# Priorities, a moved softmax scaling, two reordered products and later row factors in a two-layer hybrid transformer kernel

## The chip, the cores and the metric

The kernel runs on one core of a Trainium2 chip. The metric is the device time of one execution in microseconds (us), lower is better. A measurement of this kernel can tell about 0.2% from no change.

## The reference

The program computes two transformer layers on x of 256 rows by 1024. Each layer is a SwiGLU feed-forward block (FFN, inner width 2816), a mixer, and another FFN, each between two RMS norms and added to x. Layer 0 has the even mixer: latent attention (four heads, keys and queries of 128 + 64 rotated columns) beside a gated linear recurrence. Layer 1 has the odd mixer: differential attention, eight heads with two score maps each.

```python
for l in range(DEPTH):                                   # DEPTH = 2
    h = swiglu(rms_norm(x, g[0, 0]), w_gate, w_up, w_down); x = x + 0.5 * rms_norm(h, g[0, 1])
    h = rms_norm(x, g[1, 0])
    m = even_mixer(h, ...) if l % 2 == 0 else odd_mixer(h, ...)
    x = x + rms_norm(m, g[1, 1])
    h = swiglu(rms_norm(x, g[2, 0]), w_gate, w_up, w_down); x = x + 0.5 * rms_norm(h, g[2, 1])
# even attention: o = softmax(mask((q_nope @ k_nope.T + q_rope @ k_rope.T) * scale)) @ v
# odd attention:  p = softmax(s_0) - lam * softmax(s_1);  o = rms_norm(p @ v, g_head) * (1 - lambda_init)
```

(The listing is shortened; weights of the layers have their own names.)

## The kernel before

The 256 rows are two tiles of 128, t=0 and t=1. Every weight comes from HBM in pieces of 128 by 1024 floats (512 KB), issued by SyncE. ScalarE rounds a piece into `whi` (L269), VectorE subtracts to get the rest `wlo` (L274), and each product is three matmuls (`mm3`, L294 to L296: hi by hi, hi by lo, lo by hi). Activations are turned by TensorE (`to_T`, transposes at L403), copied as hi by ScalarE (`split`, L410) and as rest by VectorE (L411). The first product after a norm is `group_first` (matmuls at L342); it takes the second tile's turned halves as `turn1`.

Mixers are built from `group` calls, and between the pieces of weights of one group a function `pump` calls one step of the list `side`: a rope, a turn, a block of scores, a softmax. TensorE thus always has weight products around the small steps, and the order of work on each engine is the program's order, except that the scheduler places what stands in `tc.high_priority()` earlier on its engine. Before the change that holds for `split` and `post_norm` alone.

What the change touches:

- `finish` (L453) ends a block: `post_norm` of tile 0, the pieces left, `rms_x(0)`, `post_norm` of tile 1, `rms_x(1)`. `rms_x` squares a whole tile on ScalarE (L421), rounds off on VectorE (L391) and raises to the power -1/2 on GpSimd (L393). Its result r[t] is the factor with which the next block scales its first products (for instance L809 and L816 in the even mixer).
- Even mixer: `after_cq(t)` squares `cq` (L809), makes `kp` (L816) out of the same PSUM bank, `turn_cq` turns it. The table E of the recurrence comes by a DMA that ScalarE issues (L782), and ScalarE rounds it into `W` (L783). `scores(t)` makes four heads with two matmuls each, L931 (128 rows of contraction) and L932 (64 rows), then VectorE's maximum, ScalarE's exponentials and, on GpSimd, the scaling by the row sums (L940).
- Odd mixer: `after_z` scales and ropes a group's output (L1117 to L1120, rope at L717 to L720), `turn_z` turns it (L1127), `scores` makes the maps (L1144), the maxima (L1148), exponentials (L1152), the scaling of the second map on GpSimd (L1156) and the difference of the maps on VectorE (L1158), `turn_p` turns the result (L1169), `attend` multiplies by v (L1179) and applies the head norm (squares L1182, product L1188), `turn_o` turns that into the last product's operand (`to_T`).

Of the kernel before, what the change touches and what calls it, by code (L numbers as in the profile page):

```python
# [20 lines left out]
P = 128  # L21
# [162 lines left out]
def forward(ctx, tc, a):  # L184
# [268 lines left out]
    def finish(ys, gpost, half, gnext, pieces, at):  # L453


        xg = post_norm(0, ys[0], gpost, half, gnext)
        turns = turn_x(0, xg)
        for i, p in enumerate(pieces):
            if gnext is not None and i in at:
                turns[at.index(i)]()  # L460
            p()
        r0 = rms_x(0) if gnext is not None else None
        xg = post_norm(1, ys[1], gpost, half, gnext)
        if gnext is None:
            return None, None
        return [r0, rms_x(1)], turn_x(1, xg)


    def ffn_scope(block):
# [299 lines left out]
    def even(r, turn1, tab, lb, lbm):  # L769
        with ExitStack() as ex:  # L770
# [149 lines left out]
            def scores(t):  # L920
                nk = (t + 1) * P
                per = 512 // nk
                pm = one.tile([P, 4, nk], F32, name=f"pm{t}", tag=f"pm{t}")
                pms[t] = pm
                mx, nb, ssum, rs = small(4), small(4), small(4), small(4)
                for h0 in range(0, 4, per):
                    sc = ybank()
                    v = sc.rearrange("p (h k) -> p h k", h=per)
                    for i in range(per):
                        h = h0 + i  # L930
                        mm(v[:, i, :], qT[t][:, h, :], knT[:, h, :nk], start=True, stop=False)  # L931
                        mm(v[:, i, :], qrT[t][:, h, :], kpeT[:, :nk], start=False, stop=True)  # L932
                    nc.vector.memset(v[0:64, :, nk - 64:nk], -1e31)
                    nc.vector.tensor_reduce(mx[:, h0:h0 + per], v, axis=AX.X, op=ALU.max)
                    nc.vector.tensor_scalar(nb[:, h0:h0 + per], mx[:, h0:h0 + per], -scale, None, op0=ALU.mult)
                    for i in range(per):
                        h = h0 + i
                        nc.scalar.activation(pm[:, h, :], v[:, i, :], AF.Exp, scale=scale, bias=nb[:, h:h + 1], accum_out=ssum[:, h:h + 1])
                nc.vector.reciprocal(rs, ssum)
                nc.gpsimd.tensor_tensor(pm, pm, rs.unsqueeze(2).broadcast_to([P, 4, nk]), op=ALU.mult)  # L940

            def turn_p(t):
                for kt in range(t + 1):
                    pt = bank()
                    for h in range(4):
                        nc.tensor.transpose(pt[:, hsl[h]], pms[t][:, h, kt * P:(kt + 1) * P], ident)
                    p_ = m.tile([P, 512], F32, name="m", tag="m")
                    nc.scalar.copy(p_, pt)
                    pTs[t].append(p_)

            def attend(t):
# [139 lines left out]
    def odd(r, turn1, tab):  # L1091
        with ExitStack() as ex:
# [24 lines left out]
            def after_z(t, key, ps):  # L1117
                z = m.tile([P, 512], F32, name="m", tag="m")
                nc.scalar.activation(z, ps, AF.Copy, scale=r[t])
                rope(z.rearrange("p (n d) -> p n d", d=64)[:, :, 0:16], tab[:, t], 8, m)  # L1120
                zs[t, key] = z

            def turn_z(t, key):
                which, part = key
                pt = bank()
                for h in range(4):
                    nc.tensor.transpose(pt[:, hsl[h]], zs[t, key][:, hsl[h]], ident)  # L1127
                hs = slice(part * 4, part * 4 + 4)
                dst = qT[t][:, hs, :] if which == 0 else kT[:, hs, t * P:(t + 1) * P]
                nc.scalar.copy(dst, pt.rearrange("p (h n) -> p h n", h=4))  # L1130

            pms = {}

            def scores(t, part, hl):

                nk = (t + 1) * P
                n = 512 // nk
                pm = m2.tile([P, 2, n, nk], F32, name="pm", tag="pm", bufs=3)
                mx, nb, ssum, rs = small(2 * n), small(2 * n), small(2 * n), small(2 * n)
                sc = [ybank().rearrange("p (h k) -> p h k", h=n) for _ in range(2)]  # L1140
# [4 lines left out]
                for c in range(2):
                    nc.vector.memset(sc[c][0:64, :, nk - 64:nk], -1e31)
                    ms = slice(c * n, (c + 1) * n)
                    nc.vector.tensor_reduce(mx[:, ms], sc[c], axis=AX.X, op=ALU.max)  # L1148
                    nc.vector.tensor_scalar(nb[:, ms], mx[:, ms], -scale, None, op0=ALU.mult)
                    for i in range(n):  # L1150
                        q = c * n + i
                        nc.scalar.activation(pm[:, c, i, :], sc[c][:, i, :], AF.Exp, scale=scale, bias=nb[:, q:q + 1], accum_out=ssum[:, q:q + 1])  # L1152
                nc.vector.reciprocal(rs, ssum)
                rl = small(n)
                nc.vector.tensor_scalar(rl, rs[:, n:2 * n], nlam, None, op0=ALU.mult)
# [7 lines left out]
            def turn_p(t, part, hl):  # L1163
# [6 lines left out]
                nc.vector.tensor_copy(pTs[t, part][:, 0:t + 1, hl:hl + n, :], pt.rearrange("p (k h n) -> p k h n", h=n, n=P))  # L1170

            obs = {}

            def attend(t, part):
                po = (ybank, bank)[part]()
                for hl in range(4):
                    h = part * 4 + hl
                    for kt in range(t + 1):
                        mm(po[:, hsl[hl]], pTs[t, part][:, kt, hl, :], v[kt][:, h * P:(h + 1) * P], start=kt == 0, stop=kt == t)  # L1179
                ss = small(4)  # L1180
                for h in range(4):
                    nc.scalar.activation(junk[:, hsl[h]], po[:, hsl[h]], AF.Square, accum_out=ss[:, h:h + 1])  # L1182
                k2 = 1.0 / (1.0 - LI) ** 2
                ro = rpow(ss, 4, k2 / P, EPS * k2)
                o_ = m.tile([P, 512], F32, name="m", tag="m")
                for hl in range(4):
                    gs = slice((part * 4 + hl) * P, (part * 4 + hl + 1) * P)
                    nc.vector.scalar_tensor_tensor(o_[:, hsl[hl]], po[:, hsl[hl]], ro[:, hl:hl + 1], gh[:, gs], op0=ALU.mult, op1=ALU.mult)  # L1188
# [31 lines left out]
            for part in range(2):  # L1220
# [97 lines left out]
```

## Time and profile before

| | |
|---|---|
| time, median of 3 runs | 1015.85 us (1015.84 to 1016.21) |
| profiled execution, its own time | 1009.94 us |
| its span, first to last instruction | 1008.2 us |
| TensorE (PE) busy | 990.5 us, 98% |
| VectorE (DVE) busy | 788.4 us, 78% |
| ScalarE (ACT) busy | 583.4 us, 58% |
| GpSimd (POOL) busy | 52.2 us, 61 instructions |
| granted TensorE clock | 1.00 in the whole span but the last stretch (0.98) |

PE is the matmul part of TensorE and PEld its weight loads. A busy share is the mean over the span; what an engine waits for is read stretch by stretch. Tiles have the program's names, and a wait is put down to the instruction that ended it.

### The profile page before, as it was taken

What the parts mean: (1) busy time and instruction counts of PE and PEld (TensorE: products, weight loads), DVE (VectorE), ACT (ScalarE), POOL (GpSimd) and SP (SyncE); (2) the same over time, 40 slices, a digit from 0 to 9 for tenths busy, and PEclk for the clock granted to TensorE, in tenths of its full rate; (3) what the DMA queues carried; (4) which work ended last, traced back from release to release, by engine and by line L of the source; (5) the groups of instructions that cost most, each with busy time, mean ns of one, the idle gap of its engine ahead of it and who ended that gap; (6) DMA issues with size and microseconds to landing.
All of it is one profiled execution on the core that took longest, in us unless ns stands there. A gap on an engine that the chain in (4) does not pass through costs nothing.

```text
span 1008.2 us, 13275 instructions
## 1 busy us (share of the span) xinstructions
PE 990.5 (98%) x4883; PEld 825.0 (82%) x4883; DVE 788.4 (78%) x1068; ACT 583.4 (58%) x846; POOL 52.2 (5%) x61
## 2 busy tenths in 40 slices
PE   8999999999999999999999999999999999999997
PEld 6888988888788888888888889888877788889886
DVE  5998996578567899888479988865776779988852
ACT  5746584377644755657447474744665657474731
POOL 1000000021202000000010000000010210000000
PEclk9999999999999999999999999999999999999999
DMA  8938273375223883827456392737634357292701
GB/s 349 374 113 295 70 255 116 105 260 184 99 69 119 312 288 104 305 68 266 175 200 233 113 306 80 271 117 259 230 125 137 119 171 244 95 304 85 252 1 42
DMA packets 51905, 184.26 MB, mean 183 GB/s; under 512 B 6136, under 2 KB 6528, under 8 KB 51840
## 3 DMA queue, kind: packets, MB, share of 16 engines
q1 hardware_dynamic: 48960, 176.05, 50.7%
q10 hardware_dynamic: 2880, 7.37, 2.2%
q8 instruction: 38, 0.62, 0.3%
q14 instruction: 27, 0.22, 0.1%
HBM read 182.35 MB, written 1.05 MB: 182 GB/s over the span
## 4 chain that ended last, share of the span: by engine, by line
PE 89%; DVE 5%; ACT 2%; issue 1%; POOL 1%; DMA 1%; SPq 0%; POOLq 0%; DVEq 0%; ACTq 0%
PE w L294 16%; PE w L296 16%; PE w L295 16%; PE y L294 9%; PE y L296 9%; PE y L295 9%; PE w L342 7%; DVE wlo L274 2%; PE w L403 2%; PE w L1023 1%; ACT whi L269 1%; PE y L403 1%; DMA raw<-in_w_dram 1%; POOL pm L1156 1%; DVE pm L1158 0%
## 5 line engine op out<-in xcount | busy, mean ns | idle before, releaser
L269 ACT CAST whi<-raw 128x1024 fp32r<-128x1024 f32 (+2 forms) x379 | 391.4, 1049 | 268.7 <-PE y L296 90.3
L274 DVE TENSOR_TENSOR wlo<-raw,whi 128x1024 fp32r<-128x1024 f32 (+2 forms) x379 | 456.7, 1228 | 96.1 <-ACT whi L269 92.4
L294 PE MATMUL w<-whi,xThi 128*128 128x512 f32 (+1 forms) x676 | 252.7, 374 | 0.0
L296 PE MATMUL w<-whi,xTlo 128*128 128x512 f32 (+1 forms) x676 | 249.7, 369 | 0.0
L295 PE MATMUL w<-wlo,xThi 128*128 128x512 f32 (+1 forms) x676 | 249.3, 369 | 0.0
L296 PEld LDWEIGHTS w<-whi,xTlo 128*128 128x128 f32 x676 | 127.4, 188 | 21.9 <-issue 0.3
L294 PEld LDWEIGHTS w<-whi,xThi 128*128 128x128 f32 x676 | 127.5, 189 | 21.5 <-issue 1.0
L295 PEld LDWEIGHTS w<-wlo,xThi 128*128 128x128 f32 x676 | 127.5, 189 | 20.4
L294 PE MATMUL y<-whi,hThi 128*128 128x512 f32 x352 | 138.7, 394 | 0.0
L296 PE MATMUL y<-whi,hTlo 128*128 128x512 f32 x352 | 137.5, 391 | 0.0
L295 PE MATMUL y<-wlo,hThi 128*128 128x512 f32 x352 | 137.4, 390 | 0.0
L214 DVE TENSOR_TENSOR raw<-raw 128x1024 f32<-128x1024 f32 x64 | 77.4, 1220 | 1.0
L296 PEld LDWEIGHTS y<-whi,hTlo 128*128 128x128 f32 x352 | 66.1, 188 | 14.3
L295 PEld LDWEIGHTS y<-wlo,hThi 128*128 128x128 f32 x352 | 66.1, 188 | 13.5
L294 PEld LDWEIGHTS y<-whi,hThi 128*128 128x128 f32 x352 | 66.1, 188 | 13.5
L411 DVE TENSOR_TENSOR hTlo<-w,hThi 128x512 fp32r<-128x512 f32 (+1 forms) x48 | 29.8, 641 | 28.4 <-ACT hThi L410 28.0
L438 POOL TENSOR_TENSOR sm<-sm,mhalf 128x1 f32<-128x1 f32 x12 | 6.6, 550 | 701.7 <-DVE sm L436 701.7
L342 PE MATMUL w<-whi,xThi 128*128 128x512 f32 (+2 forms) x124 | 39.0, 393 | 3.9 <-ACT xThi L410 3.9
L410 ACT CAST hThi<-w 128x512 fp32r<-128x512 f32 (+1 forms) x48 | 25.1, 552 | 24.5 <-PE w L403 24.5
L342 PE MATMUL w<-wlo,xThi 128*128 128x512 f32 (+2 forms) x124 | 37.4, 387 | 0.4 <-DVE wlo L274 0.4
L342 PE MATMUL w<-whi,xTlo 128*128 128x512 f32 (+2 forms) x124 | 37.7, 385 | 0.0
L492 ACT ACTIVATE s<-w,sm 128x512 f32<-128x512 f32 (+1 forms) x40 | 25.9, 647 | 15.8 <-PE w L296 15.6
(276 smaller groups left out, 1158.1 us busy)
## 6 DMA issues: line engine op xcount, KB each, us to landing
raw<-in_w_dram SPq DMA_DIRECT2D x325, 512.0 KB, 5.6
g<-in_norm_g_dram ACTq DMA_DIRECT2D x9, 512.0 KB, 5.8
raw<-in_w_dram SPq DMA_DIRECT2D x4, 448.0 KB, 4.1
g<-in_norm_g_dram SPq DMA_DIRECT2D x2, 512.0 KB, 8.5
out_dram<-x SPq DMA_DIRECT2D x4, 256.0 KB, 2.0
E<-in_hw_dram ACTq DMA_DIRECT2D x1, 576.0 KB, 6.8
x<-in_x_dram SPq DMA_DIRECT2D x2, 256.0 KB, 3.1
x<-in_x_dram SPq DMA_DIRECT2D x1, 512.0 KB
```

Of the source, the lines that this page charges most:

```text
L214: nc.vector.tensor_tensor(to, to, what, op=ALU.add)
L269: c = nc.scalar.copy(hi[:, :w], raw[:, :w])
L274: state["lo"] = nc.vector.tensor_tensor(lo[:, :w], raw[:, :w], hi[:, :w].bitcast(F32), op=ALU.subtract)
L294: mm(ps, hi[:, j, :], rhi, start=start, stop=False, skip_group_check=again)
L295: mm(ps, hi[:, j, :], rlo, start=False, stop=False, skip_group_check=again)
L296: state["mm"] = mm(ps, lo[:, j, :], rhi, start=False, stop=stop, skip_group_check=again)
L342: state["mm"] = mm(o, lhs[:, k, :], rhs[:, i, :], start=j == 0 and k == 0, stop=j == 2 and k == KD - 1)
L403: nc.tensor.transpose(ps[:, i * P:(i + 1) * P], src[:, (b + i) * P:(b + i + 1) * P], ident)
L410: c = nc.scalar.copy(h2, ps)
L411: return c, nc.vector.tensor_tensor(lo.rearrange("p a b -> p (a b)"), ps, h2.bitcast(F32), op=ALU.subtract)
L492: nc.scalar.activation(s[:, :w], ps[:, :w], AF.Silu, scale=r[t])
L1023: mm(o, e, e, start=True, stop=True)
```

## The change

Six edits. The row factors: `finish` runs `rms_x(t)` after each half of the next block's second-tile turn, and `ffn` makes the negated factors after its first group. High priority stands on the even mixer's turn copies, query rope and softmax, and on the odd mixer's rope, turn copies, softmax and head norm. The scaling of exponentials leaves GpSimd: in the even mixer 8 ScalarE copies with a scale take the place of 2 GpSimd products, in the odd one 16 VectorE products the place of 6. The two matmuls of an even head come in alternating order from head to head. Odd attention of (t=0, part 1) comes before that of (1, 1), and so do their turns.

```diff
@@ finish
-        r0 = rms_x(0) if gnext is not None else None
         xg = post_norm(1, ys[1], gpost, half, gnext)
...
-        return [r0, rms_x(1)], turn_x(1, xg)
+        r = [None] * NT
+        def then(t, f):
+            def go():
+                f()
+                r[t] = rms_x(t)
+            return go
+        return r, [then(t, f) for t, f in enumerate(turn_x(1, xg))]
@@ ffn
-            nr = [small() for _ in range(NT)]
-            for t in range(NT):
-                nc.vector.tensor_scalar(nr[t], r[t], -1.0, None, op0=ALU.mult)
+            nr = []
...
             h = [gated(t, pu[t], s[t], w) for t in range(NT)]
+            for t in range(NT):
+                nr.append(small())
+                nc.vector.tensor_scalar(nr[t], r[t], -1.0, None, op0=ALU.mult)
@@ even, turn4 (turn_p and the query rope likewise)
-                (copy or nc.scalar.copy)(dst, pt[0:rows, :].rearrange("p (h n) -> p h n", h=4))
+                with tc.high_priority():
+                    (copy or nc.scalar.copy)(dst, pt[0:rows, :].rearrange("p (h n) -> p h n", h=4))
@@ even, scores
-                        mm(v[:, i, :], qT[t][:, h, :], knT[:, h, :nk], start=True, stop=False)
-                        mm(v[:, i, :], qrT[t][:, h, :], kpeT[:, :nk], start=False, stop=True)
+                        pair = [(qT[t][:, h, :], knT[:, h, :nk]), (qrT[t][:, h, :], kpeT[:, :nk])][::1 - 2 * (h % 2)]
+                        for j, (lhs, rhs) in enumerate(pair):
+                            mm(v[:, i, :], lhs, rhs, start=j == 0, stop=j == 1)
...
-                nc.gpsimd.tensor_tensor(pm, pm, rs.unsqueeze(2).broadcast_to([P, 4, nk]), op=ALU.mult)
+                for h in range(4):
+                    nc.scalar.activation(pm[:, h, :], pm[:, h, :], AF.Copy, scale=rs[:, h:h + 1])
@@ odd, after_z (turn_z, the whole softmax, turn_p's copy and attend's head norm likewise)
-                rope(z.rearrange("p (n d) -> p n d", d=64)[:, :, 0:16], tab[:, t], 8, m)
+                with tc.high_priority():
+                    rope(z.rearrange("p (n d) -> p n d", d=64)[:, :, 0:16], tab[:, t], 8, m)
@@ odd, scores (all of it now in the high priority block)
-                nc.gpsimd.tensor_tensor(pm[:, 1, :, :], pm[:, 1, :, :], rl.unsqueeze(2).broadcast_to([P, n, nk]), op=ALU.mult)
-                for i in range(n):
-                    nc.vector.scalar_tensor_tensor(pm[:, 0, i, :], pm[:, 0, i, :], rs[:, i:i + 1], pm[:, 1, i, :], op0=ALU.mult, op1=ALU.add)
+                    for i in range(n):
+                        nc.vector.tensor_scalar(pm[:, 1, i, :], pm[:, 1, i, :], rl[:, i:i + 1], None, op0=ALU.mult)
+                        nc.vector.scalar_tensor_tensor(pm[:, 0, i, :], pm[:, 0, i, :], rs[:, i:i + 1], pm[:, 1, i, :], op0=ALU.mult, op1=ALU.add)
@@ odd, the last steps
-            side.extend([seq((attend, 1, 1), (attend, 0, 1)), None, seq((turn_o, 1, 1)), seq((turn_o, 0, 1))])
+            side.extend([seq((attend, 0, 1), (attend, 1, 1)), None, seq((turn_o, 0, 1)), seq((turn_o, 1, 1))])
```

The order of SyncE's queue does not change. Three places of the order follow, before and then now; lines of the changed kernel have moved down by 8 to 20.

First ScalarE at the front of the even mixer, where `junk,sm<-x` is the square of `rms_x`, `junk,sm<-w,sm` that of `cq` (128x384, one for each tile), `cqThi` the turned `cq`, and E and W the recurrence's table and its rounded copy.

```order
L809 ACTIVATE junk,sm<-w,sm 128x384
L269 CAST whi<-raw 128x1024 x2
L816 ACTIVATE kp<-w,sm 128x64
L410 CAST cqThi<-y 128x384
L809 ACTIVATE junk,sm<-w,sm 128x384
L782 DMA E<-in_hw_dram 128x1152
L816 ACTIVATE kp<-w,sm 128x64
L410 CAST cqThi<-y 128x384
L809 ACTIVATE junk,sm<-w,sm 128x256
L269 CAST whi<-raw 128x1024
L783 CAST W<-E 128x1152
```

```order
L421 ACTIVATE junk,sm<-x_89 128x1024
L269 CAST whi<-raw 128x1024
L818 ACTIVATE junk,sm<-w,sm 128x384
L269 CAST whi<-raw 128x1024
L790 DMA E<-in_hw_dram 128x1152
L410 CAST cqThi<-y 128x384
L825 ACTIVATE kp<-w,sm 128x64
L421 ACTIVATE junk,sm<-x_90 128x1024
L269 CAST whi<-raw 128x1024
L818 ACTIVATE junk,sm<-w,sm 128x384
L791 CAST W<-E 128x1152
L825 ACTIVATE kp<-w,sm 128x64
```

Both squares of `rms_x` moved in here from further up, the issue of E's DMA now stands ahead of the first `kp`, and the second `kp` moved behind the cast of W.

Then TensorE in the odd mixer, at the scores of (t=1, part 1, heads 2 and 3), between `attend` of (0, 0) and the products of the last group.

```order
L1179 MATMUL y<-v_6446,pT_6448 128x128 x4
L1144 MATMUL y<-kT,qT_6444 128x256 x2
L294 MATMUL w<-whi,xThi_91 128x512
L295 MATMUL w<-wlo,xThi_91 128x512
L1144 MATMUL y<-kT,qT_6444 128x256 x2
L296 MATMUL w<-whi,xTlo_92 128x512
```

```order
L1197 MATMUL y<-v_6440,pT_6442 128x128 x4
L1160 MATMUL y<-kT,qT_6438 128x256 x4
L294 MATMUL w<-whi,xThi_91 128x512
L295 MATMUL w<-wlo,xThi_91 128x512
L296 MATMUL w<-whi,xTlo_92 128x512
```

The four score products were split by two weight matmuls and now stand together.

Last TensorE at the end of the odd mixer: `y<-whi,oThi` and `y<-whi,xThi` are the last product's matmuls by the first and the second part of the attention's output (95 and 91 belong to t=0, 97 and 93 to t=1), and L403 from `m` is `turn_o`.

```order
L403 MATMUL w<-ident,m 128x128 x4
L294 MATMUL y<-whi,oThi_97 128x512
L295 MATMUL y<-wlo,oThi_97 128x512
L296 MATMUL y<-whi,oTlo_98 128x512
L294 MATMUL y<-whi,oThi_97 128x512
L295 MATMUL y<-wlo,oThi_97 128x512
L296 MATMUL y<-whi,oTlo_98 128x512
L294 MATMUL y<-whi,xThi_91 128x512
```

```order
L403 MATMUL w<-ident,m 128x128 x4
L294 MATMUL y<-whi,oThi_95 128x512
L295 MATMUL y<-wlo,oThi_95 128x512
L296 MATMUL y<-whi,oTlo_96 128x512
L294 MATMUL y<-whi,oThi_95 128x512
L295 MATMUL y<-wlo,oThi_95 128x512
L296 MATMUL y<-whi,oTlo_96 128x512
L403 MATMUL w<-ident,m 128x128 x4
L294 MATMUL y<-whi,xThi_91 128x512
```

Before, the turn of (0, 1) was the second one (the first row above) and stood six matmuls ahead of its first use; now it is the first, with six matmuls and the other turn between it and that use.

## Rows read from the trace of the kernel before

**Rows 1.** Page, part 1: busy time of each engine.
```profile
PE 990.5 (98%) x4883; PEld 825.0 (82%) x4883; DVE 788.4 (78%) x1068; ACT 583.4 (58%) x846; POOL 52.2 (5%) x61
```

**Rows 2.** Windows: busy us (instructions) of PE, PEld, DVE, ACT, POOL; clock; DMA share; GB/s.
```profile
200.00:230.00 30.00, 30.00 (x171) 26.25 (x170) 21.51 (x39) 21.44 (x36) 9.73 (x8) 1.00 0.74 241
250.00:290.00 40.00, 40.00 (x213) 32.11 (x213) 22.20 (x54) 21.68 (x44) 5.62 (x6) 1.00 0.31 103
740.00:760.00 20.00, 17.68 (x88) 13.52 (x89) 18.42 (x48) 12.59 (x28) 4.23 (x3) 1.00 0.39 132
```

**Rows 3.** Waits of PE: total us, times, longest us.
```profile
PE w L342 <- ACT xThi L410: 3.9, 2, 2.9
PE w L1127 <- DVE sm L1149: 1.4, 1, 1.4
...
PE y L294 <- ACT xThi L410: 1.4, 1, 1.4
PE w L1169 <- DVE pm L1158: 0.9, 1, 0.9
...
PE y L931 <- DVE knT L799: 0.6, 1, 0.6
PE w L403 <- DVE m L1188: 0.6, 1, 0.6
```

**Rows 4.** Timeline of PE, even scores and attend: start, us, what [idle before].
```profile
248.56 0.46 PE L931 MATMUL y<-knT,qT 128*128 128x128 f32 x2 [0.60 <-DVE knT L799]
...
251.86 0.66 PE L798 MATMUL w<-ident,kk 128*128 128x128 f32 x4
...
255.10 0.59 PE L931 MATMUL y<-knT,qT 128*128 128x256 f32 x2
...
260.01 0.44 PE L798 MATMUL w<-ident,kk 128*128 128x128 f32 x2
...
277.85 1.95 PE L955 MATMUL w<-m,va 128*128 128x128 f32 x16
279.63 0.60 PE L798 MATMUL w<-ident,m 128*128 128x128 f32 x4
```

**Rows 5.** Timeline of ACT, front of the even mixer; last row, third FFN's start.
```profile
211.91 0.34 ACTq L782 DMA_DIRECT2D E<-in_hw_dram  x1
...
213.77 0.31 ACT L816 ACTIVATE kp<-w,sm 128x64 f32<-128x64 f32 x1 [0.92 <-DVE m L810]
...
218.74 1.16 ACT L783 CAST W<-E 128x1152 fp32r<-128x1152 f32 x1 [2.24 <-DMA E<-in_hw_dram]
...
830.75 1.06 ACT L421 ACTIVATE junk<-x 128x1024 bf16<-128x1024 f32 x1 [3.18 <-DVE x L444]
```

**Rows 6.** Timeline of PE, first matmuls of the hf group.
```profile
213.16 0.40 PE L294 MATMUL w<-whi,xThi 128*128 128x512 f32 x1
213.39 0.40 PE L295 MATMUL w<-wlo,xThi 128*128 128x512 f32 x1
```

**Rows 7.** Page, part 5, VectorE: busy us, mean ns of one, idle before.
```profile
L274 DVE TENSOR_TENSOR wlo<-raw,whi 128x1024 fp32r<-128x1024 f32 (+2 forms) x379 | 456.7, 1228 | 96.1 <-ACT whi L269 92.4
```

**Rows 8.** Timeline of POOL, odd softmax.
```profile
740.01 1.04 POOL L1156 TENSOR_TENSOR pm<-pm,sm 128x512 f32<-128x512 f32 x1 [29.11 <-PE y L1144]
```

**Rows 9.** Timeline of DVE, odd softmax, and the last head norm.
```profile
740.24 1.89 DVE L274 TENSOR_TENSOR wlo<-raw,whi 128x1024 fp32r<-128x1024 f32 x1 [0.46 <-ACT whi L269]
742.05 1.13 DVE L1158 SCALAR_TENSOR_TENSOR pm<-pm,sm 128x128 f32<-128x128 f32 x4
...
756.25 0.88 DVE L1158 SCALAR_TENSOR_TENSOR pm<-pm,sm 128x256 f32<-128x256 f32 x2 [0.93 <-POOL pm L1156]
...
801.43 1.13 DVE L1188 SCALAR_TENSOR_TENSOR m<-w,sm,gh 128x128 f32<-128x128 f32 x4 [1.12 <-POOL sm L393]
```

**Rows 10.** Timeline of PE, two odd score blocks.
```profile
770.59 1.13 PE L1144 MATMUL y<-kT,qT 64*128 64x256 f32 x8
...
777.69 1.13 PE L1144 MATMUL y<-kT,qT 64*128 64x256 f32 x4 [0.40 <-ACT pm L1152]
```

More of the change, by code (lines that the diff above doesn't have):

```diff
@@ L888, in even @@
                 nc.scalar.activation(qr[t], psr[t][:, :256], AF.Copy, scale=rq[t])
-                rope(qr[t].rearrange("p (h d) -> p h d", h=4), tab[:, t], 32, m)
+                with tc.high_priority():
+                    rope(qr[t].rearrange("p (h d) -> p h d", h=4), tab[:, t], 32, m)
             def turn_q(t):
@@ L930, in scores @@
                         h = h0 + i
-                        mm(v[:, i, :], qT[t][:, h, :], knT[:, h, :nk], start=True, stop=False)
-                        mm(v[:, i, :], qrT[t][:, h, :], kpeT[:, :nk], start=False, stop=True)
[L933 to L938, printed above, removed]
+                        pair = [(qT[t][:, h, :], knT[:, h, :nk]), (qrT[t][:, h, :], kpeT[:, :nk])][::1 - 2 * (h % 2)]
+                        for j, (lhs, rhs) in enumerate(pair):
+                            mm(v[:, i, :], lhs, rhs, start=j == 0, stop=j == 1)
+                    with tc.high_priority():
+                        nc.vector.memset(v[0:64, :, nk - 64:nk], -1e31)
+                        nc.vector.tensor_reduce(mx[:, h0:h0 + per], v, axis=AX.X, op=ALU.max)
+                        nc.vector.tensor_scalar(nb[:, h0:h0 + per], mx[:, h0:h0 + per], -scale, None, op0=ALU.mult)
+                        for i in range(per):
+                            h = h0 + i
+                            nc.scalar.activation(pm[:, h, :], v[:, i, :], AF.Exp, scale=scale, bias=nb[:, h:h + 1], accum_out=ssum[:, h:h + 1])
                 nc.vector.reciprocal(rs, ssum)
-                nc.gpsimd.tensor_tensor(pm, pm, rs.unsqueeze(2).broadcast_to([P, 4, nk]), op=ALU.mult)
+                for h in range(4):
+                    nc.scalar.activation(pm[:, h, :], pm[:, h, :], AF.Copy, scale=rs[:, h:h + 1])
             def turn_p(t):
@@ L947, in turn_p @@
                     p_ = m.tile([P, 512], F32, name="m", tag="m")
-                    nc.scalar.copy(p_, pt)
+                    with tc.high_priority():
+                        nc.scalar.copy(p_, pt)
                     pTs[t].append(p_)
@@ L1119, in after_z @@
                 nc.scalar.activation(z, ps, AF.Copy, scale=r[t])
-                rope(z.rearrange("p (n d) -> p n d", d=64)[:, :, 0:16], tab[:, t], 8, m)
+                with tc.high_priority():
+                    rope(z.rearrange("p (n d) -> p n d", d=64)[:, :, 0:16], tab[:, t], 8, m)
                 zs[t, key] = z
@@ L1129, in turn_z @@
                 dst = qT[t][:, hs, :] if which == 0 else kT[:, hs, t * P:(t + 1) * P]
-                nc.scalar.copy(dst, pt.rearrange("p (h n) -> p h n", h=4))
+                with tc.high_priority():
+                    nc.scalar.copy(dst, pt.rearrange("p (h n) -> p h n", h=4))
             pms = {}
@@ L1144, in scores @@
                         mm(sc[c][:, i, :], qT[t][cs, part * 4 + hl + i, :], kT[cs, part * 4 + hl + i, :nk], start=True, stop=True)
[L1145 to L1149, printed above, removed]
-                    for i in range(n):
[L1151 to L1155, printed above, removed]
-                nc.gpsimd.tensor_tensor(pm[:, 1, :, :], pm[:, 1, :, :], rl.unsqueeze(2).broadcast_to([P, n, nk]), op=ALU.mult)
-                for i in range(n):
-                    nc.vector.scalar_tensor_tensor(pm[:, 0, i, :], pm[:, 0, i, :], rs[:, i:i + 1], pm[:, 1, i, :], op0=ALU.mult, op1=ALU.add)
+                with tc.high_priority():
+                    for c in range(2):
+                        nc.vector.memset(sc[c][0:64, :, nk - 64:nk], -1e31)
+                        ms = slice(c * n, (c + 1) * n)
+                        nc.vector.tensor_reduce(mx[:, ms], sc[c], axis=AX.X, op=ALU.max)
+                        nc.vector.tensor_scalar(nb[:, ms], mx[:, ms], -scale, None, op0=ALU.mult)
+                        for i in range(n):
+                            q = c * n + i
+                            nc.scalar.activation(pm[:, c, i, :], sc[c][:, i, :], AF.Exp, scale=scale, bias=nb[:, q:q + 1], accum_out=ssum[:, q:q + 1])
+                    nc.vector.reciprocal(rs, ssum)
+                    rl = small(n)
+                    nc.vector.tensor_scalar(rl, rs[:, n:2 * n], nlam, None, op0=ALU.mult)
+                    for i in range(n):
+                        nc.vector.tensor_scalar(pm[:, 1, i, :], pm[:, 1, i, :], rl[:, i:i + 1], None, op0=ALU.mult)
+                        nc.vector.scalar_tensor_tensor(pm[:, 0, i, :], pm[:, 0, i, :], rs[:, i:i + 1], pm[:, 1, i, :], op0=ALU.mult, op1=ALU.add)
                 pms[t, part, hl] = pm
@@ L1169, in turn_p @@
                         nc.tensor.transpose(pt[:, (kt * n + i) * P:(kt * n + i + 1) * P], pm[:, 0, i, kt * P:(kt + 1) * P], ident)
-                nc.vector.tensor_copy(pTs[t, part][:, 0:t + 1, hl:hl + n, :], pt.rearrange("p (k h n) -> p k h n", h=n, n=P))
+                with tc.high_priority():
+                    nc.vector.tensor_copy(pTs[t, part][:, 0:t + 1, hl:hl + n, :], pt.rearrange("p (k h n) -> p k h n", h=n, n=P))
             obs = {}
@@ L1179, in attend @@
                         mm(po[:, hsl[hl]], pTs[t, part][:, kt, hl, :], v[kt][:, h * P:(h + 1) * P], start=kt == 0, stop=kt == t)
[L1180 to L1188, printed above, removed]
+                with tc.high_priority():
+                    ss = small(4)
+                    for h in range(4):
+                        nc.scalar.activation(junk[:, hsl[h]], po[:, hsl[h]], AF.Square, accum_out=ss[:, h:h + 1])
+                    k2 = 1.0 / (1.0 - LI) ** 2
+                    ro = rpow(ss, 4, k2 / P, EPS * k2)
+                    o_ = m.tile([P, 512], F32, name="m", tag="m")
+                    for hl in range(4):
+                        gs = slice((part * 4 + hl) * P, (part * 4 + hl + 1) * P)
+                        nc.vector.scalar_tensor_tensor(o_[:, hsl[hl]], po[:, hsl[hl]], ro[:, hl:hl + 1], gh[:, gs], op0=ALU.mult, op1=ALU.mult)
                 obs[t, part] = o_
```

## Prediction

> **What bounds the kernel now.** First the busy times: TensorE is busy 990.5 of 1008.2 us, VectorE 788, ScalarE 583, GpSimd 52 [rows 1]. So TensorE bounds the kernel nearly everywhere, and a change that leaves the number of matmuls alone can at most take away the 17.7 us in which TensorE stands still, plus what its own instructions lose between one another. Then the windows: where a group of weights runs smoothly the idle time is nil, 30.00 of 30 us at the front of the even mixer, with the clock at 1.00; in the odd mixer's softmax stretch TensorE is busy 17.68 of 20 us while VectorE is at 18.42 [rows 2]. Then TensorE's waits by releaser: 3.9 us for `xThi` in two pieces (2.9 of it at the program's start, which the change does not touch, so 1.0 at the start of the third FFN), 1.4 for a roped tile behind the softmax, 1.4 for the last turn, 0.9 for the probabilities, 0.6 for `knT`, 0.6 for the head norm [rows 3]. Most of the rest of the 17.7 us is the program's start and end. What the change can reach is thus about 6 us of waits, and some matmul overhead.
>
> **The sum, part by part.** All terms are against the profiled execution, 1009.94 us with 1.7 us around its span; the median of the runs, 1015.85, is 5.9 higher, and I carry that difference over unchanged.
>
> *Alternating score matmuls, even mixer.* The t=0 block of 16 records takes 251.86 − 248.56 = 3.30 us, 0.206 each; 16 records of one shape, all 128 rows of contraction, take 279.63 − 277.85 = 1.78 us, 0.111 each [rows 4]. The block changes between 128 and 64 rows with every pair of records, 8 times with the change at its end, so (3.30 − 1.78) / 8 = 0.19 us for one change of shape. The t=1 block takes 260.01 − 255.10 = 4.91 us [rows 4]; with twice the columns 16 × 0.22 + 8 × 0.19 = 5.0 would be expected, which agrees. With the order alternating by head (128, 64, 64, 128, 128 and so on) 4 changes are left in each block: 8 × 0.19 = 1.5 us less, all on TensorE's path. Nought, if the loss belongs to something else than the shape.
>
> *Row factors later, even mixer's front: a new wait.* Both squares of `rms_x`, 1.06 us each [rows 5], come after the turn on ScalarE. r[0] is ready only after its square, VectorE's round-off and GpSimd's power; `cq`'s square waits for r[0], and behind that on ScalarE's queue stands the DMA of E. By the new order this DMA is ahead of both `kp`, one `cqThi` and the second `cq` square, but behind one `rms_x` square and the wait for r[0]: I put its issue at 211.0, against 211.91 before. The cast of W started 218.74 − 211.91 = 6.8 us after the issue, and its row says that it waited 2.24 us for that DMA [rows 5]. That hid, because the second `kp` had run at 213.77, 5 us ahead of it. Now the second `kp` is queued behind the cast, and its bank is what TensorE needs for the t=1 half of the hf group. Issue 211.0 + 6.8 = 217.8, cast 1.16, `kp` 0.31 [rows 5]: 219.3. TensorE starts the hf group at 213.16 with 0.23 a matmul [rows 6]; 17 t=0 matmuls now stand ahead of the first t=1 matmul, with two turns of three transposes at 0.11 [rows 4], so it wants the bank at 213.16 + 3.9 + 0.7 = 217.7. That is a stall of 1.6 us, and I add 0.2 for banks that wait for the late square: loss 1.8. The bounds: 0.3, if the DMA lands 1.5 us sooner, and 3, if r[0] holds the issue until 212.2. The DMA engines are busy 0.74 of this stretch [rows 2], so a later landing is a rival below. SyncE's queue keeps its order; on GpSimd's only the two powers move, and nothing else waits in it there.
>
> *Scaling in the even mixer to ScalarE.* Two GpSimd products go, eight scaled copies of 128 or 256 columns come on ScalarE. The nearest rows are `kp`, 64 columns in 0.31 us, and W, 1152 columns in 1.16 [rows 5], so up to 0.5 each, 4 us in all. ScalarE is busy 21.68 of 40 us from 250 to 290 [rows 2], while TensorE does weight products; I take nothing. If that cover went, the two blocks' turns would be late by up to 4 × 0.5 = 2 us each.
>
> *FFN starts.* At the FFN behind the even mixer the turns come about one cast nearer to `post_norm`: −0.4 (0 to −1). At the third FFN `rms_x` (1.06 us [rows 5]) leaves ScalarE's way to `xThi`, whose wait was 1.0 us [rows 3]; but the turns of the second tile also come earlier in TensorE's order than `post_norm` may feed them: +0.3 (−0.3 to +1.0). The other block ends show no wait and get none.
>
> *Odd softmax, 740 to 757.* GpSimd's product is a link between the exponentials and VectorE's difference: VectorE idles 0.93 us for it [rows 9], TensorE 0.9 in its wake, and 1.4 for a rope that stood behind the softmax [rows 3]. The products go to VectorE, eight of 128x128 and eight of 128x256. By the nearest rows, the differences, 1.13 / 4 = 0.28 and 0.88 / 2 = 0.44 us [rows 9], the three blocks (of six) in this stretch add 4 × 0.28 + 4 × 0.44 = 2.9 us to an engine that had 1.6 us idle in 20 [rows 2]. What it gets back: a `wlo` took 1.89 us [rows 9] while GpSimd's product of 1.04 us ran [rows 8], against a mean of 1.23 [rows 7], so 0.7 each time. Priority puts the ropes first, which removes the 1.4, and lets the probabilities come later. So VectorE is the limit with or without GpSimd, and I take 0 for the two waits (−1.0 to +1.5).
>
> The Trainium skill (Perfetto Trace Analysis, Optimizing Scalar/DVE Operations) says that where VectorE is saturated, offloading work to ScalarE or even GpSimd may make sense, which speaks against this part, and adds that between GpSimd and VectorE it might not help since they share a port. The first half is rival 2, 0.4 us in place of the sum's 2.9; the second half is what the 1.89 us row shows.
>
> *Odd scores at 777.* Four records of a block run at 777.69 after a wait of 0.40, split off from their other four; these four take 1.13 us, as long as a whole block of eight at 770.59, 1.13 [rows 10]. Together they pay it once: 0.4 + 1.1 = 1.5 us. It needs the exponentials that free their bank to come earlier, which priority gives. 0 to 1.6.
>
> *Head norm at 790.* The wait of 0.6 [rows 3] goes, since squares and products now come ahead of the weights' casts: 0.6 (0 to 1.0).
>
> *Last turns.* The turn that is used first was the second. Now six matmuls and a turn, 6 × 0.23 + 0.4 = 1.8 us, lie between it and its use, against a wait of 1.4 [rows 3]. Its cast, and `xTlo` behind two `wlo`, still follow the head norms, the second of which starts at 801.43 [rows 9]; that may leave 0.2. So 1.2 (0.3 to 1.5).
>
> The wait for `knT` stays: VectorE's order ahead of it is the old one.
>
> Sum: 1.5 − 1.8 − 0.4 + 0.3 + 1.5 + 0.6 + 1.2 = **2.9 us faster**: 1007.0 for a profiled execution, 1012.95 for the median, as a forecast 1013.0.
>
> **Rivals.**
> 1. *Slower: E's DMA.* One mechanism, W's cast ahead of the second `kp` on ScalarE. For: the order has it so, and the DMA had no slack before. If E takes twice as long (13.6 us) behind pieces of weights, the stall is 1.6 + 6.8 = 8.4 and the sum 4.7 − 8.4 − 0.2 = −3.9: 1019.7. It decides from a landing 2.9 us later than assumed, and shows as slower from 4.9. Against: the 6.8 us came in the same traffic. Chance 0.07.
> 2. *VectorE becomes the bound in the odd mixer.* Products and priority delay `wlo` and the turned probabilities; the gains at 777 and 790 (2.1) and 0.4 of the last turns do not come: 2.9 − 2.5 = 0.4, 1015.4. For: it is 92% busy from 740 to 760. Against: 0.7 back per product, and no rise of its share elsewhere. Chance 0.22.
> 3. *More: no stall at the front*, because E lands early, and 1.2 of the waits from 740 to 757 gone: 2.9 + 1.6 + 1.2 = 5.7, 1010.1. Chance 0.18.
> 4. *The shape order does nothing*, since each new pair costs by itself: 2.9 − 1.5 = 1.4, 1014.4. Chance 0.08.
>
> **How the numbers follow.** The forecast has 0.45, and the time is its own, 1013.0. The range runs from rival 3 to no gain, 1009.5 to 1016.0; outside lie rival 1 and the edges. A measurement can tell 0.2%, 2.0 us. Faster than that: most of the forecast (0.40), rival 3 (0.18), some of 4 and 2: 0.62. Within: 0.29. Slower: rival 1 and a bad end of rival 2, 0.09.
>
> **What would show it.** Right: the t=0 score block at about 2.5 us and t=1 at about 4.1; a wait of TensorE of 1 to 2 us near 217 for the second `kp`; eight odd score records in one row near 775; no wait for the head norm near 790, and under 0.5 us at the last turns; VectorE at 19 of 20 us from 740 to 760. Wrong: no wait near 217, or one of over 4 us; waits for `wlo` in the odd mixer; score blocks as long as before; a granted clock under 1.00 where it was 1.00.

## The result and the profile after

| | before | changed |
|---|---|---|
| median, first comparison (6 runs each) | 1015.45 us (1012.8 to 1016.21) | 1006.77 us (1006.18 to 1009.64) |
| ratio, 95% interval | | 0.9925 (0.9908 to 0.9943) |
| median, measured again later (e5; 19 and 5 runs) | 1012.14 us | 1007.62 us |
| ratio, 95% interval | | 0.9953 (0.9937 to 0.997) |
| profiled execution, span | 1009.94, 1008.2 us | 1009.64, 1007.8 us |

The change made the kernel faster, by 8.7 us in the first comparison and by 4.5 in the second. The forecast was 2.9 faster, a time of 1013.0, and 1006.77 lies below its range. The two profiled executions differ by only 0.3 us, so neither of the two gains is seen in them as it stands.

Busy times of the changed kernel (page, part 1, as [rows 1]) have hardly moved; only GpSimd has less to do.

```profile
PE 991.2 (98%) x4883; PEld 826.5 (82%) x4883; DVE 789.4 (78%) x1084; ACT 585.0 (58%) x854; POOL 47.8 (5%) x53
```

TensorE's waits of the changed kernel (total, times, longest us), as [rows 3]:

```profile
PE w L342 <- ACT xThi L410: 3.4, 2, 2.8
PE w L1186 <- DVE pm L1175: 2.4, 2, 2.2
...
PE y L296 <- DVE oTlo L411: 1.0, 1, 1.0
PE w L1037 <- DVE A L1039: 0.7, 1, 0.7
PE y L943 <- DVE knT L808: 0.6, 1, 0.6
...
PE w L403 <- DVE pT L1188: 0.2, 1, 0.2
PE y L296 <- DVE xTlo L411: 0.2, 1, 0.2
```

The waits for the roped tile and for the last turn's `xThi` are gone, as is the one at 832, the start of the FFN behind the odd mixer. (That is the fourth of the program's four FFNs; the prediction calls it the third.) The 3.4 us for `xThi` are 2.8 at the program's start and 0.6 at the start of the real third FFN, at 533. New are 2.2 us for probabilities (L1186) and 1.0 for `oTlo`. On TensorE's timeline, the hf group's second-tile start, the two score blocks, and the odd mixer, as [rows 4, 10]:

```profile
218.79 0.49 PE L403 MATMUL y<-ident,m 128*128 128x128 f32 x3
219.03 0.48 PE L294 MATMUL w<-whi,xThi 128*128 128x512 f32 x1
...
250.30 0.46 PE L943 MATMUL y<-knT,qT 128*128 128x128 f32 x2 [0.64 <-DVE knT L808]
...
257.74 0.60 PE L943 MATMUL y<-knT,qT 128*128 128x256 f32 x2
...
261.98 0.60 PE L806 MATMUL w<-ident,kk 128*128 128x128 f32 x4
...
759.79 0.30 PE L1186 MATMUL w<-ident,pm 128*128 128x128 f32 x1 [2.17 <-DVE pm L1175]
...
778.44 1.14 PE L1160 MATMUL y<-kT,qT 64*128 64x256 f32 x8
...
791.41 0.66 PE L403 MATMUL w<-ident,m 128*128 128x128 f32 x4 [0.24 <-DVE pT L1188]
...
795.48 0.50 PE L296 MATMUL y<-whi,oTlo 128*128 128x512 f32 x1 [0.97 <-DVE oTlo L411]
...
806.68 0.50 PE L296 MATMUL y<-whi,xTlo 128*128 128x512 f32 x1 [0.22 <-DVE xTlo L411]
```

The eight odd score records at 778.44 now run in one piece, the last turn waits 0.22. ScalarE's front of the even mixer, as [rows 5]:

```profile
211.65 0.34 ACTq L790 DMA_DIRECT2D E<-in_hw_dram  x1
...
217.25 1.16 ACT L791 CAST W<-E 128x1152 fp32r<-128x1152 f32 x1
218.50 0.31 ACT L825 ACTIVATE kp<-w,sm 128x64 f32<-128x64 f32 x1
```

E landed by 217.25 at the latest, 5.6 us after its issue, and the second `kp` ended at 218.81, just ahead of the 219.03 at which TensorE came to its bank. And VectorE ahead of the 2.2 us wait:

```profile
757.62 0.22 DVE L725 TENSOR_TENSOR rp<-m,roped 128x64 f32<-128x64 f32 x1
...
758.43 0.35 DVE L1174 TENSOR_SCALAR pm<-pm,sm 128x256 f32<-128x256 f32 x1
758.69 0.22 DVE L725 TENSOR_TENSOR rp<-m,roped 128x64 f32<-128x64 f32 x1
...
759.16 0.48 DVE L1175 SCALAR_TENSOR_TENSOR pm<-pm,sm 128x256 f32<-128x256 f32 x1
```

Ropes stand ahead of the maps' scaling (L1174) and again between it and the difference (L1175) that TensorE waits for; L725 is one of a rope's products.

That the two traces differ by 0.3 and not by 4.5 us is in part the clock (1.00 is 2.4 GHz, 0.50 is 1.2). In the changed kernel's trace the granted clock fell inside the even scores, here in windows as [rows 2]; in before's it did not.

```profile
250.00:255.00 5.00, 4.70 (x23) 4.06 (x24) 3.11 (x6) 1.68 (x3) 0.00 (x0) 0.79 0.77 265
255.00:260.00 5.00, 5.00 (x19) 3.64 (x19) 0.18 (x1) 4.99 (x16) 0.00 (x0) 0.87 0.10 38
```

At the program's start the clock column misleads. Before's windows show 1.00 there, but its first products behind the start's wait run slowly; the changed kernel (windows 10 to 20: 0.55 and 0.77) only stays slow for longer. TensorE in before, then the second of these pairs in the changed kernel:

```profile
9.76 1.22 PE L342 MATMUL w<-whi,xThi 128*128 128x512 f32 x2 [2.94 <-ACT xThi L410]
...
13.95 0.74 PE L342 MATMUL w<-whi,xThi 128*128 128x512 f32 x2
```

```profile
13.84 1.20 PE L342 MATMUL w<-whi,xThi 128*128 128x512 f32 x2
```

From the first product to the hundredth matmul record behind it before takes 24.45 us and the changed kernel 26.01.

### The profile page after: what moved, and what is told of

It is laid out like the page before. It is cut to its first block, busy times and chain, and to the rows that moved or that the text cites. A ratio compares the mean times of both kernels' runs of the same rounds, so it can differ in the third digit from the quotient of the medians.

```text
span 1007.8 us, 13278 instructions
## 1 busy us (share of the span) xinstructions
PE 991.2 (98%) x4883; PEld 826.5 (82%) x4883; DVE 789.4 (78%) x1084; ACT 585.0 (58%) x854; POOL 47.8 (5%) x53
## 4 chain that ended last, share of the span: by engine, by line
PE 89%; DVE 6%; DMA 1%; ACT 1%; issue 1%; POOL 0%; SPq 0%; DVEq 0%; POOLq 0%; ACTq 0%
PE w L294 16%; PE w L296 16%; PE w L295 16%; PE y L296 9%; PE y L295 9%; PE y L294 9%; PE w L342 7%; DVE wlo L274 2%; PE w L403 2%; DMA raw<-in_w_dram 1%; PE w L1037 1%; PE y L403 1%; PE y L943 1%; DVE sm L1165 1%; ACT whi L269 1%
## 5 line engine op out<-in xcount | busy, mean ns | idle before, releaser
L269 ACT CAST whi<-raw 128x1024 fp32r<-128x1024 f32 (+2 forms) x379 | 391.5, 1049 | 257.9 <-PE w L296 79.9
```

Of the source, the lines that this page charges most:

```text
L269: c = nc.scalar.copy(hi[:, :w], raw[:, :w])
```

## The experiments

The gains below are against runs of the kernel before that were taken beside each experiment, on the same chip. The table under the experiments tells where in the program they arise.

**e1, the kernel before again.**

> The kernel before, unchanged, to see the granted clock of its timed runs. Known: its one profiled execution took 1009.94 us with the clock at 1.000, its timed runs 1012.8 to 1016.2; the changed kernel's runs took 1006.2 to 1009.6 with mean clocks of 0.993 to 0.998. Theory C (clock): of the 8.7 us, some 3.4 are waits and shape changes and the rest is the clock, which falls to half for some us after waits that the change removes; then most runs here show mean clocks of 0.985 to 0.993 with spans of 1011 to 1014, and a run at 1.000 has a span near 1008. Theory W (waits): the clock is as in the changed kernel, 0.993 to 0.998, and the spans are above 1010 all the same, because waits differ from run to run.

1012.01 against 1011.73 us: the same; here the kernel before is 3.7 us faster than it was first. Mean clocks 0.992 to 1.000, most of them 0.995 or 0.996. Neither theory holds as put: the clock is as in the changed kernel, but it does sort the runs. In all the experiments together the kernel before was run 99 times: the 22 runs with a mean clock up to 0.994 have a median of 1013.9 us, the 62 at 0.995 to 0.997 of 1011.7, the 15 above of 1011.0.

**e2, e3, e4: one part each.** e2 has only the edits in `finish` and `ffn`, e3 only those of the even mixer, e4 only those of the odd mixer, each as the diff above has them.

> Only the later row factors. In the trace of the changed kernel the second kp came in time (no wait near 217) and the FFN starts changed by -1 to +1 us. Theory C: within 1 us of before, mean clocks as before. Theory W: 0.3 to 1 us faster from the third FFN's start, less the 0.6 us wait that the changed kernel has at 533.

> Only the even mixer's edits (priority, alternating score matmuls, scaling on ScalarE). Both theories: 1.3 us faster, all from the score blocks (3.30 to 2.6 and 4.91 to 4.2 us). Theory C adds that the mean clock stays as in the kernel before, since the wait for knT stays.

> Only the odd mixer's edits (priority, scaling on VectorE, last turns). The traces give 3.2 us less waiting from 740 to 815. Theory C: 5 to 7 us faster in the timed runs, with a mean clock some 0.003 to 0.006 higher than the kernel before shows in e1. Theory W: 3.2 us faster at the same clock.

e2: 0.7 us faster (ratio 0.9992, 0.9983 to 1.0), which both theories allow. e3: 1.2 (0.9987, 0.9978 to 0.9995), as both said. e4: 1.5 (0.9981, 0.997 to 0.9993), with a mean clock up to 0.994 in 7 of 12 runs: behind its 2.2 us wait near 760 the clock fell in the profile to 0.88 and 0.78 of full in two 5 us stretches. Theory C said 5 to 7 us for e4, and lost; theory W's 3.2 missed too, in the trace by 1.6 us that the fall cost.

**e5, the changed kernel again; e8, without the row factors** (`finish` and `ffn` as before).

> The changed kernel, unchanged, beside the kernel before. The three parts alone gave 0.7, 1.2 and 1.5 us, 3.4 in sum, and the mean clock was 0.992 to 1.000 with the edits and without, so theory C of the first runs has lost. Theory A (the parts add up; what was seen first, 8.7 us, holds a difference of the kernel before between chips or hours, 1015.4 there against 1011.7 here): 3 to 4.5 us faster, ratio 0.9955 to 0.997. Theory I (the parts work together, each alone leaves a wait that the next one takes over): 7 to 9 us faster, ratio near 0.992.

> The changed kernel without the later row factors. Theory A: 0 to 1 us slower than the changed kernel (0.7 alone), the score of the even front 0.3 us better, the third FFN's wait of 1 us back, and the 0.6 us wait near 533 gone. Theory I: 2 us slower or more.

e5: 4.5 us faster, theory A. e8: 1007.45, the same as e5: inside the changed kernel the later row factors are worth nothing that can be told. Against what was expected of e8, the wait of 1 us at the fourth FFN did not come back.

**e6, no priority on the odd rope.**

```diff
-                with tc.high_priority():
-                    rope(z.rearrange("p (n d) -> p n d", d=64)[:, :, 0:16], tab[:, t], 8, m)
+                rope(z.rearrange("p (n d) -> p n d", d=64)[:, :, 0:16], tab[:, t], 8, m)
```

> The changed kernel without the priority on the odd mixer's rope alone. The changed kernel's largest new wait is 2.17 us near 760 for the probabilities of (1, 0, heads 2 and 3): VectorE has two ropes ahead of their scaling. Theory V (VectorE is the limit there, the order only shifts the wait): this kernel loses the 2.2 us wait and gets back 1.4 us at a rope'd tile's turn near 750: within 1 us of the changed kernel. Theory O (the order makes the wait): 1.5 to 2.5 us faster than the changed kernel.

1005.24 us, 2.4 faster than e5: theory O. In place of 2.2 us TensorE waits 0.3 for probabilities, and 0.4, not 1.4, for the roped tile:

```profile
PE w L1141 <- DVE sm L1169: 0.4, 1, 0.4
PE w L1185 <- DVE pm L1174: 0.3, 1, 0.3
```

**e7, the odd scaling back on GpSimd; e10, the scaling alone.** e7 puts one GpSimd product back in place of the second map's VectorE ones and keeps all else of the change; e10 is the kernel before with only the products exchanged, in both mixers.

> The changed kernel with the odd mixer's scaling back on GpSimd (one product for the second map instead of two or four on VectorE), priorities kept. Theory V: VectorE has 2.9 us more room from 740 to 757 but waits for GpSimd's products and its wlo are stretched beside them: within 1 us of the changed kernel. Rival, that the scaling on VectorE is worth something itself: 1 to 2 us slower than the changed kernel, with VectorE waiting 0.9 us at a time for GpSimd.

> The kernel before with only the scaling moved off GpSimd (ScalarE in the even mixer, VectorE in the odd), no priority and nothing reordered. Theory V: VectorE is the limit from 740 to 757, so 0 to 1 us faster than before in the odd mixer, nothing in the even one. Rival (GpSimd is what costs there): 2 us faster or more, with fewer runs above 1013.5.

e7: 1009.25, 1.6 us slower than e5: the rival. e10: 1.1 faster than before (0.9989, 0.9979 to 0.9999), which lies between its two theories. In e10's trace the odd mixer is 1.3 us shorter: 0.5 up to the score block at 770, the rest at the next score block and the head norm. So the scaling is worth something by itself. Four of TensorE's waits in e7's odd mixer, which has more and smaller ones, and then the one that e10 has for probabilities:

```profile
745.47 0.30 PE L1186 MATMUL w<-ident,pm 128*128 128x128 f32 x1 [0.85 <-ACT pm L1169]
...
757.38 0.30 PE L1186 MATMUL w<-ident,pm 128*128 128x128 f32 x1 [0.87 <-ACT m L1133]
...
777.15 1.13 PE L1160 MATMUL y<-kT,qT 64*128 64x256 f32 x6 [0.47 <-ACT pm L1169]
...
790.91 0.33 PE L403 MATMUL w<-ident,m 128*128 128x128 f32 x1 [0.97 <-DVE pT L1188]
```

```profile
759.34 0.30 PE L1170 MATMUL w<-ident,pm 128*128 128x128 f32 x1 [1.79 <-ACT whi L269]
```

**e9, e6 with the even mixer's `G` product on VectorE.**

```diff
-                nc.gpsimd.tensor_tensor(g_, g_, gout, op=ALU.mult)
+                nc.vector.tensor_tensor(g_, g_, gout, op=ALU.mult)
```

> The changed kernel without the rope's priority, and with the product G times gout (even mixer) on VectorE instead of GpSimd. In some profiles two VectorE products of 0.28 us took 1.35 us each near 306 while GpSimd's G product ran, and TensorE then waited 0.7 us for A; in others GpSimd's product took 3.4 instead of 2.6 us and VectorE went ahead. Theory L (the two engines shut each other out, and which one wins changes from run to run): no 0.7 us wait at the second use of A, 0.5 to 1.5 us faster than e6, so 1004 us. Rival: the two products cost VectorE 0.7 us each there, and the wait stays: same as e6.

1003.70 us (1003.4 to 1004.05), ratio 0.9914 (0.99 to 0.9928): 1.5 us below e6, which was measured on another chip, and without the wait of 0.7 at the second use of `A`. That is theory L, and with it a version that beats both kernels.

**e11, e12, the kernel before, one profiled run each.**

> The kernel before again, for a look at one of its slower runs: 13 of 65 runs took over 1013.5 us, all with a mean clock of 0.991 to 0.994. Theory D (a fall of the clock behind a wait in the odd mixer or behind the knT wait): if this run is such a one, a stretch of 5 to 10 us at a clock near 0.5 to 0.8 stands right behind one of the waits at 248, 294, 750, 757, 777, 790, 806 or 832. Rival: it stands at the start only. In a run at 1010 to 1012: a fall at the start or none.

> The same once more, a second look at the kernel before. Theory D: a run above 1013.5 us shows a fall of the clock right behind one of its waits of 0.6 us or more; rival: at the start only. A run at 1010 to 1012 shows a fall at the start or none.

e11: 1012.07 us, clock fallen at the start only. e12: 1014.79 us, one of the longer runs. Windows of e12, then TensorE's timeline:

```profile
10.00:15.00 5.00, 4.52 (x12) 3.10 (x13) 5.00 (x6) 3.87 (x5) 0.00 (x0) 0.51 1.03 419
250.00:255.00 5.00, 5.00 (x21) 3.83 (x22) 2.53 (x4) 0.52 (x1) 0.00 (x0) 0.75 0.78 277
255.00:260.00 5.00, 5.00 (x15) 3.79 (x13) 0.45 (x3) 4.11 (x12) 1.04 (x1) 0.57 0.01 2
```

```profile
249.98 0.46 PE L931 MATMUL y<-knT,qT 128*128 128x128 f32 x2 [0.59 <-DVE knT L799]
...
252.04 0.49 PE L932 MATMUL y<-kpeT,qrT 64*128 64x128 f32 x2
...
253.18 0.79 PE L932 MATMUL y<-kpeT,qrT 64*128 64x128 f32 x2
```

The clock fell at the start, and again from about 252.4 on, 2.5 us behind the wait for `knT` and inside the score block: the same pair of records takes 0.79 us in place of 0.49. Theory D's sign is there; whether the wait or the score block brings the fall, this trace can't tell.

**e13, e14: keys turned ahead of the queries**, in the kernel before and in e9.

```diff
-seq((turn_q, 0), (turn_q, 1), (turn_kn, 0), (turn_kn, 1))
+seq((turn_kn, 0), (turn_q, 0), (turn_kn, 1), (turn_q, 1))
```

> The kernel before with the keys turned ahead of the queries in the even mixer, so that knT(0) is copied by VectorE one wlo (1.2 us) earlier and TensorE's wait of 0.6 us ahead of the scores goes. Theory D (the clock falls behind that wait): no wait for knT and no fall near 250 in the profile, runs above 1013.5 us (14 of 84 before) become rare, the median 0.7 to 1.5 us lower. Rival S (the score block itself, with matmuls of few columns and changes of shape, brings the fall): the wait goes, 0.7 us faster, but one run in six is still above 1013 with a clock of 0.994 or less.

> The fastest variant so far (the changed kernel, no priority on the odd rope, G on VectorE, 1003.70 us) with the keys turned ahead of the queries. Both theories: 0.5 to 0.8 us faster, 1003.0; theory D: all runs within 1 us of each other.

e13: 0.8 us faster (0.9991, 0.9981 to 1.0001), no wait for `knT`, and none of 11 runs with a mean clock under 0.995. That is what theory D expects, but at the rate of before (22 of 99) eleven such runs come by chance about one time in sixteen; and 1.2 us came back at the next FFN as a wait for `wlo`. Nor does it decide against rival S: e3, e6, e7 and e9 kept the wait for `knT` and have the alternating score matmuls, and of their 31 runs one alone had such a clock (e7's 1012.71 us). So the order of the score matmuls may matter more than the wait; it is not a cure, for the changed kernel's profile has the alternating order and a fall. e14: 1003.42 us (1002.91 to 1004.99), ratio 0.9924 (0.9912 to 0.9937): the same as e9, where 0.5 to 0.8 less was expected, and its runs spread over 2.1 us, where theory D said 1.

**Where the time went.** For seven stretches: by how much a trace is longer (+) or shorter (−) than that of before, in us. It is the start of the same `whi` cast (L269, counted from 0 at the program's start: numbers 80, 98, 106, 113, 160, 280 and 340) in the trace, less its start in before's, and the difference to the column on the left. The heads give before's times.

| | to 190 | 243, even front | 285, scores | 325, out | 429, FFN | 723, two FFNs | 895, odd and FFN |
|---|---|---|---|---|---|---|---|
| changed | 1.44 | 0.30 | 0.06 | 0.04 | −0.18 | 1.17 | −3.17 |
| e5, changed again | 2.17 | 0.35 | −1.54 | 1.18 | −0.12 | 0.02 | −3.14 |
| e1, before again | 0.78 | −0.01 | 0.01 | 1.14 | 0.02 | 0.10 | −0.01 |
| e12, before again | 1.43 | 0.00 | 3.09 | 0.01 | 0.06 | 0.28 | −0.01 |
| e2, row factors | −0.15 | 0.30 | 0.01 | 1.12 | −0.19 | 0.00 | −0.58 |
| e3, even | 2.14 | 0.00 | −1.54 | 0.05 | 0.10 | 0.10 | 0.40 |
| e4, odd | −0.06 | 0.00 | 0.01 | 1.15 | 0.06 | 0.41 | −1.51 |
| e8, no row factors | 0.60 | 0.00 | −1.54 | 1.19 | 0.38 | 0.00 | −3.07 |
| e6, no rope priority | 0.90 | 0.35 | −1.54 | 1.19 | −0.19 | 0.04 | −5.18 |
| e7, scaling on GpSimd | 0.76 | 0.34 | −1.54 | 1.17 | −0.13 | 0.00 | −1.74 |
| e10, scaling only | 1.02 | −0.01 | 1.43 | 0.05 | 0.05 | 0.47 | −1.33 |
| e9 | 0.22 | 0.35 | −1.56 | 0.07 | −0.16 | 0.36 | −5.14 |
| e11, before again | 0.85 | 0.01 | 0.02 | 1.15 | 0.08 | −0.01 | 0.03 |
| e13, keys first | −0.42 | 0.01 | −0.81 | 1.10 | 1.25 | 0.03 | 0.01 |
| e14, keys first in e9 | 0.73 | 0.36 | −2.41 | 0.03 | −0.17 | 0.03 | −5.17 |

What repeats is the edits: −1.54 for the scores, +0.3 for the later row factors at the front and −0.2 at the FFN behind, −3.1 for the odd mixer with the FFN after it, of which the scaling alone makes −1.3 (e10) and the rest −1.7 (e7). Sum −4.5, the gain of e5. What comes and goes from run to run is the rest: the start (the first product comes at 8.9 to 11.0 us, and how long it stays slow behind that differs by 1.6), 1.1 to 1.2 us in "out", the 1.17 in one trace before 723 (its profile shows `whi` waiting for a weight's DMA), and the falls of the clock, +3.09 in the scores of e12, 1.43 in e10's, 1.54 + 0.06 = 1.60 in the changed kernel's, and −1.51 instead of −3.1 in e4's odd mixer.

## Why the prediction was wrong

- **The failed step: "the median of the runs, 1015.85, is 5.9 higher, and I carry that difference over unchanged."** It was taken for a fixed addition, the same for both kernels. It did not carry over: the changed kernel's median lies 2.9 us below its own profiled execution, and before's only 1.5 to 2.2 above its own in the later comparisons (1011.4 to 1012.1, on three chips). What the traces show in its place are things that one execution has and another has not: a slow start that costs 0.6 to 1.6 us more than in before's profile, falls of the clock worth 1.4 to 3.1 in the scores, and a wait worth 1.1 to 1.2 in "out". Before's profile had none of these three, the changed kernel's had the first two. The edits are 4.5 of the 8.7 us, by e5 and by the sum above. Where the other 4.2 come from stays open. Five of before's first six runs took 1014.0 to 1016.2 us, and their clocks are not on record. Of the 99 later runs only 18 took over 1013.5, and none as much as 1015.84, which the three runs that the prediction started from all reach; so the falls that were seen later, at the rate seen later, don't explain them.
- **Score matmuls, 1.5:** right, 1.54 with what stands close behind the blocks. The t=1 block takes 4.24 us instead of 4.91; the t=0 block, under a fallen clock in this trace, takes 2.64 instead of 3.30 in e3. Rival 4 is out.
- **The front, −1.8:** the order came as said, the stall did not: −0.3, without a listed wait. The second `kp` was ready 0.2 us ahead of its need, and the need was where the prediction had put it. E's DMA took 5.6 us, not 6.8, and was issued, with the trace's later start of 1.4 taken off, at 210.2, not 211.0. The 6.8 was from the slow end: in the traces without the later row factors E took 5.5 to 6.9 us, in those with them 5.2 to 5.6. Rival 1 is out.
- **FFN starts, −0.1 in sum:** 0.2 faster behind the even mixer, and about 1.1 at the fourth FFN (the prediction's third), whose wait of 1.0 is gone. It is gone in e2, with the row factors alone, and in e4, with the odd edits alone: either does.
- **Odd softmax, 0:** right in the changed kernel, 0.1 lost from 720 to 770, but for a wrong reason, so by luck. "VectorE is the limit with or without GpSimd" does not hold: with the same work e6 gains 2.0 us by the order alone. Over the same stretch of 20 us VectorE is busy 19.0 us in the changed kernel (first row) with TensorE at 17.6, and 19.9 in e6 (second row) with TensorE at 19.4. The priority on the ropes made the 2.2 us wait.

```profile
743.00:763.00 20.00, 17.63 (x88) 13.60 (x88) 19.01 (x57) 12.10 (x28) 0.00 (x0) 1.00 0.45 141
```

```profile
741.00:761.00 20.00, 19.37 (x102) 15.08 (x100) 19.89 (x57) 14.20 (x30) 0.00 (x0) 1.00 0.38 124
```

- **Odd scores 1.5 and head norm 0.6:** both came, but the wait of 1.0 for `oTlo` at 795, which the prediction did not have, took half of it back; from the score block at 770.59 to the `attend` of the last part the changed kernel gained 1.0.
- **Last turns, 1.2:** 1.2. The wait that is left is 0.22, as thought.
- **Rival 2 (VectorE bound):** the gains that it took away came. A delay of the probabilities by priority, as it said, came as well, but e6 shows that the order made it and not the load. The rule behind it, in the Trainium skill (Perfetto Trace Analysis, Optimizing Scalar/DVE Operations), to offload a saturated VectorE, does not decide here: at 18.4 of 20 us busy VectorE took over GpSimd's products and the odd mixer became 1.3 us shorter (e10).
- **Rival 3** was nearest: no stall at the front. Its 1.2 us from the waits of 740 to 757 came only in e6.

So the sum of the edits, 2.9, should have been 4.5; the range would have held the gain of the second comparison, and missed the first time because the 5.9 did not carry over.

## What to carry to other kernels

Before a gain of under 1% is carried from a profile to a median, ask why the profiled execution and the timed runs differ: take the granted clock of each run, and profile a run that is longer than the median as well. A priority is a move past other work: give it to the steps that TensorE waits for next, and look at what now stands behind them (the rope's priority cost 2 us). Take a small product off an engine that only links two others, even when the receiver looks full.

## What was not expected of the hardware

**VectorE and GpSimd shut each other out, and who wins is not fixed.** The even mixer's `G` product on GpSimd and VectorE's L1006 run side by side in all 14 traces that have `G` on GpSimd. In the profile of before, VectorE's products took 0.28 us and one `wlo` 2.17, and two GpSimd products 3.38 us together (VectorE, then GpSimd):

```profile
303.95 0.28 DVE L1006 TENSOR_TENSOR E<-E,hkT 128x128 f32<-128x128 f32 x1
...
304.56 0.28 DVE L1006 TENSOR_TENSOR E<-E,hqT 128x128 f32<-128x128 f32 x1
...
306.13 2.17 DVE L274 TENSOR_TENSOR wlo<-raw,whi 128x1024 fp32r<-128x1024 f32 x1
```

```profile
303.84 3.38 POOL L1058 TENSOR_TENSOR G<-G,gout 128x512 f32<-128x512 f32 x2 [1.17 <-ACT G L1057]
```

In e1 two of VectorE's products took 1.36 and 1.35 us, GpSimd's 2.61, and TensorE then waited for A:

```profile
304.74 1.36 DVE L1006 TENSOR_TENSOR E<-E,hkT 128x128 f32<-128x128 f32 x1
306.03 1.35 DVE L1006 TENSOR_TENSOR E<-E,hqT 128x128 f32<-128x128 f32 x1
```

```profile
304.63 2.61 POOL L1058 TENSOR_TENSOR G<-G,gout 128x512 f32<-128x512 f32 x2 [1.17 <-ACT G L1057]
```

```profile
PE w L1066 <- DVE A L1025: 0.7, 1, 0.7
```

That is the 1.1 to 1.2 us of column "out": nine of the 14 traces have the pair of 1.36 and 1.35 us and with it that loss, the other five have neither. With the product on VectorE (e9, e14) it was in neither trace. The Trainium skill (SBUF — State Buffer, Who interferes with whom) says that a VectorE instruction with two SBUF inputs contends with a GpSimd one that reads SBUF, and that the order of issue decides who blocks. The rows agree with the first half. They don't show the second, as far as start times in a profile can: in both traces GpSimd's product starts 0.11 us ahead of a VectorE product (303.84 and 303.95, 304.63 and 304.74), and the winner differs.

**The clock falls behind short waits, but not always.** It was at 0.50 for some us around the end of the start's wait in 12 of 16 profiles. It also fell behind a 0.6 us wait for `knT` followed by the score block (e10, e12, the changed kernel), at a cost of 1.4 to 3.1 us, more than the wait ahead of it, and behind 2.2 us near 760 (e4), at a cost of 1.6. The same waits without a fall stand in other traces, so they do not decide alone.

**A window's 1.00 can hide a slow start.** In e3 all windows show 1.00 and its mean clock is 0.999, yet from the first product to the hundredth record behind it e3 takes 25.55 us, before 24.45.
